# A hybrid decoder step on one core: the last tile's products stand beside the gate matrices, and its retrieval is decoded in small steps

## The chip, the cores and the metric

The kernel runs on one core of one Trainium2 chip. The metric is the device time of one execution in microseconds (us), from the first instruction to the last with what lies around them; three executions of the kernel before are given, and one more that was taken with the profiler on. Engines are called as in the profile: PE is the matrix engine, DVE the vector engine, ACT the scalar engine, POOL the general engine that also issues indirect gathers, SP the engine whose queue issues most plain transfers.

## The reference, cut to what matters

One layer of a decoder is computed for 512 prompt tokens (with 16 learned tokens ahead of them) and for 32 sample tokens. A recurrent group of heads and a window-attention group are computed from one projection, joined, projected by `w_out` and added to x. Then follows the part that matters here, the retrieval of experts (`peer`), and a last norm:

```python
x = x + concat(y_rw, y_at) @ w_out
h = rmsnorm(x, norm2_g)
q = (h @ w_query).reshape(T, 8, 2, 128)            # 8 heads, 2 halves of the key
s = einsum('thcd,cnd->thcn', q, sub_keys)          # 128 scores for each half
s1, i1 = top_k(s[:, :, 0], 16); s2, i2 = top_k(s[:, :, 1], 16)
cand, cidx = s1[..., :, None] + s2[..., None, :], i1[..., :, None] * 128 + i2[..., None, :]
top, sel = top_k(cand, 16)                         # over the 256 pairs of each head
idx, gate = cidx[sel], softmax(top)                # 128 experts for each token, of 16384
act = gelu(h . expert_u[idx]) * gate
y = x + sum_k act[k] * expert_v[idx[k]]            # then rmsnorm(y, final_norm_g)
```

Every matrix is float32: `expert_u` and `expert_v` have 16384 rows of 4 KB each.

## The kernel before, in words

**Stages.** The tokens are 4 tiles of 128 prompt tokens and one of 32 sample tokens. From 0 to about 1110 us runs the front: projections, the recurrent scan, attention, and the heads of tiles 0 to 2 and of the sample. Two ways of retrieval are used. Tiles 1 and 2 (256 tokens) go through **all** experts densely, in 128 blocks of 128 experts; each token's gate is zero for the experts that it didn't choose. Tile 0, the sample and tile 3 (the last) fetch their chosen rows with gathers: 128 gathers of `expert_u` rows and 128 of `expert_v` rows per tile, 512 KB each (32 and 32 for the sample).

**Gates** (1119 to 1238 us, `gates`). The gate matrix (128 tokens by 128 by 128 experts) of each dense tile is made in 16 steps of 8 tokens. DVE and ACT make one-hot rows (uH, uL, vH), PE multiplies them (8 products a step, L1401), ACT copies the results out. The first tile's matrices go to DRAM (gscr), the second's stay (gA, gB) but for a quarter.

**Dense blocks** (1238 to 2184 us). For each block of 128 experts PE transposes its rows (L1446), multiplies them with the hidden states in three products of high and low parts (L1460, L1461, L1463: 24 matmuls), and after gelu (ACT) and gates (DVE) multiplies the result with `expert_v` into PSUM (L1477 to L1479: 24 matmuls). POOL makes the low part vL of `expert_v` once in each block (L1453), so that vL numbers the blocks in a trace. DVE makes uL twice, the gate product twice, and aL once for each block.

**The last tile** (`late`, a generator). Four steps of `w_out` (L1522), the norm, 8 transposes, then 8 steps with two products of `w_query` and two of the scores each (L1544, L1547); after each second one `two_heads` decodes a group of 2 heads: the 16 best of 128 by MAX8, FIND_INDEX8 and MATCH_REPLACE8 on DVE, tables on DVE and POOL. Two steps are traced behind each dense block, from block 0. The four groups done, tile 3's 256 gathers are appended to the work at the side.

**Gathers at the side** (`experts`, L1032, and `beside`). A generator issues a gather on POOL into one of 5 buffers; two gathers later DVE takes the row: for `expert_u` a dot product (`gat<-gat,h` or `gat<-gat,lx`), for `expert_v` an addition (`x<-gat,act,x`). Behind each gate step 0.8 of such a step is traced, behind each dense block up to 3; at the end of the program what is left of them.

**Order.** The framework sorts each engine's instructions at build time by a model of their times, with the tracing order as priority. Each engine then runs its own list in that order and waits where an operand or a buffer isn't ready. A pool of tiles that is opened where an earlier one lay waits for the users of that memory; sb and pp (front) and dn and dp (gates and dense blocks) are such pools. After the dense blocks, `finish` norms and stores tiles 1 and 2, and the last gathers' tile.

Of the kernel before, what the change touches and what calls it, by code (L numbers as in the profile page):

```python
# [11 lines left out]
F32 = mybir.dt.float32  # L12
# [5 lines left out]
PSUM = bass.MemoryType.PSUM  # L18
# [95 lines left out]
def hymba_step(ctx, tc, x_prompt, x_sample, cache_k, cache_v, state_wkv, state_shift, meta, norm1_g, w_in, mu, w0,  # L114
# [3 lines left out]
    A, G, T, DM = nc.scalar, nc.gpsimd, nc.tensor, nc.sync  # L118
# [22 lines left out]
    hscr_s = dr.tile([32, D], F32, name="hscr_s")  # L141
    xscr_s = dr.tile([32, D], F32, name="xscr_s")
    sscr = dr.tile([32, 16, 128], F32, name="sscr")
    yscr = dr.tile([128, 8, 128], F32, name="yscr")
    gscr = dr.tile([16, 128, 128, 8], F32, name="gscr")
    gscr2 = dr.tile([128, 4, 128, 8], F32, name="gscr2")
# [748 lines left out]
    def top16(src, vals, idx):  # L895

        V.max(vals[:, 0:8], src)
        V.max_index(idx[:, 0:8], vals[:, 0:8], src)
        V.match_replace(src, vals[:, 0:8], src, -3.0e38)
        V.max(vals[:, 8:16], src)  # L900
        V.max_index(idx[:, 8:16], vals[:, 8:16], src)

    held = []
# [64 lines left out]
                        eq=("ce", 1), res=("res", 2), d1=("d1", 2))[kind], shape, dt)  # L968

    def two_heads(sc, dst, tile_):  # L970

        vals, idx = tile_("vals", [128, 2, 2, 16]), tile_("idx", [128, 2, 2, 16], U32)
        for j in range(4):
            top16(sc[:, j, :], vals[:, j // 2, j % 2, :], idx[:, j // 2, j % 2, :])
        idf = idx.bitcast(F32)
        V.tensor_copy(idf, idx)
        cand = tile_("cand", [128, 2, 72])  # L980
        for c0, a0_, na, nb in ((0, 0, 2, 16), (32, 2, 2, 8), (48, 4, 4, 4), (64, 8, 8, 1)):
            G.tensor_tensor(cand[:, :, c0:c0 + na * nb].rearrange("p h (a b) -> p h a b", b=nb),
                            bc(vals[:, :, 0, a0_:a0_ + na].unsqueeze(3), [128, 2, na, nb]),
                            bc(vals[:, :, 1, 0:nb].unsqueeze(2), [128, 2, na, nb]), OP.add)

        def sm(dt=F32):
            return tile_("sm", [128, 2, 16], dt)
        top, sel, d1 = tile_("top", [128, 2, 16]), tile_("sel", [128, 2, 16], U32), tile_("d1", [128, 2, 16])
        for h in range(2):
            top16(cand[:, h, :], top[:, h, :], sel[:, h, :])  # L990
        pf = sm()
        V.tensor_copy(pf, sel)
        m = sm()
        V.tensor_scalar(m, pf, 32.0, 8.0, OP.is_ge, OP.mult)
        for lim, x in ((48.0, 4.0), (64.0, 3.0)):
            t = sm()
            V.tensor_scalar(t, pf, lim, x, OP.is_ge, OP.mult)
            V.tensor_tensor(m, m, t, OP.add)
        mu_ = sm(U32)
        V.tensor_scalar(mu_, m, -1.0, 15.0, OP.mult, OP.add)  # L1000
        V.tensor_tensor(sel, sel, mu_, OP.bitwise_and)
        bf = mu_.bitcast(F32)
        V.tensor_copy(bf, sel)
        G.tensor_copy(d1[:, :, 0:1], idf[:, :, 0, 0:1])
        G.tensor_tensor(d1[:, :, 1:16], idf[:, :, 0, 1:16], idf[:, :, 0, 0:15], OP.subtract)
        full = [128, 2, 16, 16]
        res = dst[0:2] if len(dst) == 3 else [tile_("res", [128, 32]) for _ in range(2)]
        for r, tab, pos, op, val in ((res[0], first, pf, OP.is_le, d1), (res[1], iota16, bf, OP.is_equal, idf[:, :, 1, :])):
            eq = tile_("eq", full)
            V.tensor_tensor(eq, bc(tab.unsqueeze(1).unsqueeze(1), full), bc(pos.unsqueeze(3), full), op)  # L1010
            G.tensor_tensor(eq, eq, bc(val.unsqueeze(2), full), OP.mult)
            V.tensor_reduce(r.rearrange("p (h k) -> p h k", h=2), eq, AX.X, OP.add)
        if len(dst) == 2:
            V.scalar_tensor_tensor(dst[0], res[0], 128.0, res[1], OP.mult, OP.add)
        gate = dst[-1].rearrange("p (a b) -> p a b", a=2)
        V.tensor_tensor(gate, top, bc(top[:, :, 0:1], [128, 2, 16]), OP.subtract)
        A.activation(gate, gate, AF.Exp)
        su, rd = small(2, "R"), small(2, "R")
        V.tensor_reduce(su, gate, AX.X, OP.add)
        V.reciprocal(rd, su)  # L1020
        V.tensor_tensor(gate, gate, bc(rd.unsqueeze(2), [128, 2, 16]), OP.mult)
# [139 lines left out]
    with ExitStack() as px:  # L1161
# [43 lines left out]
        def put(src, dst):  # L1205

            A.copy(dst[0], src)
            V.tensor_tensor(dst[1], src, dst[0].bitcast(F32), OP.subtract)
# [68 lines left out]
            project(blk, wt, ws, jps(), lambda k: [t[:, k, :] for t in hA], NA, _t(pj, "own", 2, [128, NA]),  # L1277
                    _t(pj, "po", 3, [128, NA]), 0)

    sb = fr.enter_context(tc.tile_pool(name="sb", bufs=1))  # L1280
    pp = fr.enter_context(tc.tile_pool(name="pp", bufs=1, space=PSUM))
    def meta_wkv():
        r = rwkv_prep(40, 16)
        wkv_local(r)
# [95 lines left out]
    def gates(its, sel, ps, put):  # L1380


        i1T, i2T, gaT = sel
        its, iot = its
        ib = dt_("aH", 2, [128, 2, 128], BF16)
        for c, x in enumerate((i1T, i2T)):
            A.copy(ib[:, c], x)
        for n, t8 in enumerate(range(0, 128, 8)):
            ob = dt_("uL", 2, [128, 128, GA], BF16)
            o0, o1 = dt_("uH", 2, [128, 8, 128]), dt_("vH", 2, [128, 8, 128])  # L1390
            V.tensor_tensor(o0.rearrange("p t j -> p j t"), its, bc(ib[:, 0, t8:t8 + 8].unsqueeze(1), [128, 128, 8]), OP.is_equal)
            V.tensor_tensor(ob, its[:, :, 0:GA], bc(ib[:, 1, t8:t8 + GA].unsqueeze(1), [128, 128, GA]), OP.is_equal)
            for q0 in (0, 4):
                p = ps()
                for q in range(q0, q0 + 4):
                    t = slice(t8 + q, t8 + q + 1)
                    if q < GA:
                        A.mul(o1[:, q, :], ob[:, :, q], gaT[:, t])
                    else:
                        V.tensor_scalar(o1[:, q, :], iot, i2T[:, t], gaT[:, t], OP.is_equal, OP.mult)  # L1400
                    T.matmul(p[:, 128 * (q - q0):128 * (q - q0) + 128], o0[:, q, :], o1[:, q, :], start=True, stop=True)  # L1401
                put(t8 + q0, p)
            with tc.issue_after(marks[-1]):
                beside(RATE_G)


    ND = 256
    dn = ctx.enter_context(tc.tile_pool(name="dn", bufs=1))
    dp = ctx.enter_context(tc.tile_pool(name="dp", bufs=1, space=PSUM))

    def dt_(tag, bufs, shape, dt=F32):
        return _t(dn, tag, bufs, shape, dt)
# [95 lines left out]
    def late():  # L1508
        x2 = dt_("lx", 1, [128, D])
        DM.dma_start(x2, x_prompt[0, 384:512, :])  # L1510
        yT = dt_("ly", 1, [128, 8, 128])
        DM.dma_start(yT, yscr)

        def weights_of(w, n):
            wt = dt_("uv", UV, [128, 8, 256])
            DM.dma_start(wt, w[0][:, 256 * n:256 * n + 256].rearrange("(k p) c -> p k c", p=128))
            return wt
        for n in range(4):
            wt = weights_of(w_out, n)
            p = dps()[:, 0:256]  # L1520
            for k in range(8):
                T.matmul(p, yT[:, k, :], wt[:, k, :], start=(k == 0), stop=(k == 7))  # L1522
            o = x2[:, 256 * n:256 * n + 256]
            V.tensor_tensor(o, o, p, OP.add)
            yield True
        gj = dt_("uv", UV, [128, 2, D])
        DM.dma_start(gj[:, 0], norm2_g[0].partition_broadcast(128))
        DM.dma_start(xscr[3], x2)
        rms(x2, x2, 128, gj[:, 0], "E", gj[:, 1])
        yield True  # L1530
        h2T = dt_("ly", 1, [128, 8, 128])

        def put(half, p):
            A.copy(h2T[:, 4 * half:4 * half + 4, :], p)
        h_transposed(x2, 128, put, dps)
        yield True
        for g in range(4):
            sc = dt_("lsc", 1, [128, 4, 128])
            for j0 in (0, 2):
                wt = weights_of(w_query, 2 * g + j0 // 2)  # L1540
                for j in range(2):
                    p = dps()
                    for k in range(8):
                        T.matmul(p[:, 0:128], wt[:, k, 128 * j:128 * j + 128], h2T[:, k, :], start=(k == 0), stop=(k == 7))  # L1544
                    qT = dt_("lq", 1, [128, 128])
                    A.copy(qT, p[:, 0:128])
                    T.matmul(p[:, 128:256], qT, skT[:, j, :], start=True, stop=True)  # L1547
                    A.copy(sc[:, j0 + j, :], p[:, 128:256])  # L1548
                yield True
            two_heads(sc, [x[:, 32 * g:32 * g + 32] for x in pl1], late_tile)  # L1550
        side.append(tile_experts(3, *pl1, x2))

    for n in range(AHEAD):
# [4 lines left out]
    sels = [sel_transposed(0, dps, dt_("selT", 1, [128, 3, 128])), sel_transposed(1, dps, dt_("lsc", 1, [128, 3, 128]))]  # L1558
    gates(its, sels[0], dps, stage)
    gates(its, sels[1], dps, keep)  # L1560
    gl = {}

    def gate_of(j):
# [68 lines left out]
```

## Time and profile before

| | us |
|---|---|
| median of 3 runs | 2198.62 |
| lowest, highest | 2183.69, 2198.69 |
| profiled execution, its own time | 2204.76 |
| span in the profile | 2203.0 |
| PE busy | 1839.1 (83%) |
| DVE busy | 1690.4 (77%) |
| POOL busy | 1249.2 (57%) |
| ACT busy | 867.3 (39%) |

A page of the profile gives the busy share of each engine in 40 slices of the span (55 us each), the clock that PE was granted, and what the transfers moved. Views of the trace give an engine's instructions in order of time, the busy time of all engines in a stretch, or groups by line; the number in brackets in a timeline is how long the engine stood idle just before, and what ended that. In all of them an instruction on DVE has line 126, since one helper records them; its tiles tell which it is.

### The profile page before, as it was taken

Reading aid. Unit: us, or ns where it says so; the run is one execution under the profiler, and the core shown is the slowest. Engines: PE = TensorE matmul, PEld = TensorE weight load, DVE = VectorE, ACT = ScalarE, POOL = GpSimd, SP = SyncE. Lnnn points to the kernel's source line nnn. Section 1 sums busy time; section 2 is a strip of 40 time slices with the busy share of each in tenths; the row PEclk is TensorE's granted clock in tenths of the full one; section 3 lists DMA queues with packets and bytes.
Section 4 is the critical chain, followed back from the end, with each engine's and each line's share of the span. In section 5 each row is a group of like instructions: output and inputs, shape, how many; then the busy total and the mean of one; then the engine's idle time right before and its main releaser. Section 6 shows DMA issues by size and latency. Waiting matters only on the chain.

```text
span 2203.0 us, 37197 instructions
## 1 busy us (share of the span) xinstructions
PE 1839.1 (83%) x13915; PEld 1716.0 (78%) x13915; DVE 1690.4 (77%) x3393; ACT 867.3 (39%) x1963; POOL 1249.2 (57%) x963
## 2 busy tenths in 40 slices
PE   5899975585759868996547897899999999999996
PEld 5888974473647747886446787899999999999995
DVE  5543436788788788799989879997778787787887
ACT  6554422211224313323169634334444444444443
POOL 0110103878784676565624546867667776767774
PEclk9999996556755659898778999999999999999998
DMA  7532473687786789996757887799899999999995
GB/s 222 157 101 84 122 191 102 208 288 248 230 273 199 231 273 318 285 317 222 243 163 242 299 313 239 270 326 340 334 330 331 342 326 336 335 325 343 325 330 178
DMA packets 310154, 569.51 MB, mean 259 GB/s; under 512 B 32787, under 2 KB 194565, under 8 KB 309830
## 3 DMA queue, kind: packets, MB, share of 16 engines
q0 software_dynamic: 84048, 305.70, 39.7%
q1 hardware_dynamic: 225926, 261.43, 36.6%
q8 instruction: 110, 1.80, 0.3%
q14 instruction: 70, 0.57, 0.1%
HBM read 543.07 MB, written 24.60 MB: 258 GB/s over the span
## 4 chain that ended last, share of the span: by engine, by line
PE 51%; DVE 22%; DMA 10%; issue 9%; POOL 5%; ACT 3%; SPq 0%; DVEq 0%; POOLq 0%; ACTq 0%
DVE gat L126 5%; PE acc L1478 5%; PE w L1460 5%; PE w L1461 5%; PE w L1463 5%; PE acc L1479 5%; PE acc L1477 5%; PE w L1446 4%; POOL gat L1032 4%; DVE x L126 4%; PE pD L218 3%; DMA gat<-in_expert_v_dram,ei 3%; PE ps L218 2%; DMA wst<-in_w_query_dram 2%; DMA gat<-in_expert_u_dram,ei 2%
## 5 line engine op out<-in xcount | busy, mean ns | idle before, releaser
L126 DVE SCALAR_TENSOR_TENSOR x<-gat,act,x 128x1024 f32<-128x1024 f32 x287 | 427.9, 1491 | 24.7 <-DMA gat<-in_expert_v_dram,ei 23.4
L1032 POOL DMA_INDIRECT gat<-in_expert_u_dram,ei x256 | 343.0, 1340 | 158.8 <-DVE pre L126 75.7
L1032 POOL DMA_INDIRECT gat<-in_expert_v_dram,ei x256 | 294.4, 1150 | 193.6 <-DVE x L126 73.1
L1453 POOL TENSOR_TENSOR vL<-uv,vH 128x1024 fp32r<-128x1024 f32 x128 | 322.5, 2519 | 56.1 <-ACT vH L1452 54.3
L1478 PE MATMUL acc<-aL,vH 128*128 128x256 f32 x1024 | 290.7, 289 | 17.2 <-DVE aL L126 17.1
L1479 PE MATMUL acc<-aH,vL 128*128 128x256 f32 x1024 | 289.3, 287 | 0.0
L1477 PE MATMUL acc<-aH,vH 128*128 128x256 f32 x1024 | 280.5, 295 | 5.3 <-ACT aH L1469 5.3
L1460 PE MATMUL w<-dhH,uH 128*128 128x256 f32 x1024 | 252.5, 284 | 0.2 <-ACT lsc L1548 0.2
L1461 PE MATMUL w<-dhL,uH 128*128 128x256 f32 x1024 | 251.6, 283 | 0.0
L126 DVE CUSTOM_DVE_ANT_0 gat<-gat,h 128x1024 f32<-128x1024 f32 x160 | 213.5, 1343 | 49.6 <-DMA gat<-in_expert_u_dram,ei 47.8
L1478 PEld LDWEIGHTS acc<-aL,vH 128*128 128x128 f32 x1024 | 200.6, 196 | 19.3 <-DVE aL L126 19.3
L126 DVE CUSTOM_DVE_ANT_0 gat<-gat,lx 128x1024 f32<-128x1024 f32 x128 | 214.4, 1686 | 0.0
L1452 ACT CAST vH<-uv 128x1024 fp32r<-128x1024 f32 x128 | 134.6, 1051 | 195.7 <-issue 131.8
L1479 PEld LDWEIGHTS acc<-aH,vL 128*128 128x128 f32 x1024 | 200.6, 196 | 0.0
L1460 PEld LDWEIGHTS w<-dhH,uH 128*128 128x128 f32 x1024 | 196.9, 192 | 0.5 <-ACT lsc L1548 0.4
L1461 PEld LDWEIGHTS w<-dhL,uH 128*128 128x128 f32 x1024 | 196.8, 192 | 0.1
L1477 PEld LDWEIGHTS acc<-aH,vH 128*128 128x128 f32 x1024 | 188.0, 193 | 6.0 <-ACT aH L1469 5.9
L126 DVE TENSOR_TENSOR uL<-w,uH 128x512 fp32r<-128x512 f32 x256 | 167.6, 681 | 3.0 <-ACT uH L1448 3.0
L126 DVE TENSOR_TENSOR w<-w,gl 128x128 f32<-128x128 f32 x128 | 50.5, 395 | 143.3 <-ACT w L1464 143.2
L1463 PE MATMUL w<-dhH,uL 128*128 128x256 f32 x1024 | 151.9, 287 | 2.8 <-DVE uL L126 2.8
L1448 ACT CAST uH<-w 128x512 fp32r<-128x512 f32 x256 | 139.1, 592 | 8.4 <-PE w L1446 3.0
L1446 PE MATMUL w<-ident,uv 128*128 128x128 f32 x1024 | 141.4, 273 | 0.0
(575 smaller groups left out, 4113.8 us busy)
## 6 DMA issues: line engine op xcount, KB each, us to landing
uv<-in_expert_u_dram SPq DMA_DIRECT2D x128, 512.0 KB, 4.5
uv<-in_expert_v_dram SPq DMA_DIRECT2D x128, 512.0 KB, 5.9
wst<-in_w_query_dram SPq DMA_DIRECT2D x48, 512.0 KB, 5.5
wst<-in_w_out_dram SPq DMA_DIRECT2D x24, 512.0 KB, 6.9
wst<-in_w_in_dram SPq DMA_DIRECT2D x20, 512.0 KB, 4.4
h2T<-in_w_in_dram SPq DMA_DIRECT2D x20, 512.0 KB, 4.1
gscr<-uv SPq DMA_DIRECT2D x10, 1024.0 KB, 6.5
gl<-gscr SPq DMA_DIRECT2D x16, 512.0 KB, 7.4
```

The costliest lines, as they stand in the source:

```text
L126: r = getattr(nc.vector, name)(*args, **kw)
L1032: G.indirect_dma_start(out=r, out_offset=None, in_=w[0], in_offset=bass.IndirectOffsetOnAxis(ap=ei[:, k:k + 1], axis=0))
L1446: T.transpose(p[:, q, :], un[:, 128 * k:128 * k + 128], ident)
L1448: A.copy(uH[:, ks, :], p)
L1452: A.copy(vH, vn)
L1453: G.tensor_tensor(vL, vn, vH.bitcast(F32), OP.subtract)
L1460: T.matmul(pre, uH[:, k, :], hH[:, k, :], start=(k == 0), stop=False)
L1461: T.matmul(pre, uH[:, k, :], hL[:, k, :], start=False, stop=False)
L1463: T.matmul(pre, uL[:, k, :], hH[:, k, :], start=False, stop=(k == 7))
L1477: T.matmul(o, vH[:, ds_], aH, start=(j == 0 and d % 2 == 0), stop=False, skip_group_check=True)
L1478: T.matmul(o, vH[:, ds_], aL, start=False, stop=False, skip_group_check=True)
L1479: T.matmul(o, vL[:, ds_], aH, start=False, stop=(j == 127), skip_group_check=True)
```

## The change

Three things. First, `late` is one step for each step of `gates`, so that its products stand beside the 16 steps of the first gate matrix; the scores go to buffers of the tag gl, and from there to DRAM (lscr, 256 KB a group). Second, decoding is now `late_heads`: a group's scores are read back from lscr, and `head_steps` decodes them in pieces (7 yields a group, 28 in all), two pieces behind each dense block; then tile 3's gathers follow as before. Third, pools sb, pp, dn and dp wait tile by tile for the memory that they take over.

```diff
+    lscr = dr.tile([4, 128, 4, 128], F32, name="lscr")
...
     def two_heads(sc, dst, tile_):
+        for _ in head_steps(sc, dst, tile_):
+            pass
+
+    def head_steps(sc, dst, tile_):
...
             top16(sc[:, j, :], vals[:, j // 2, j % 2, :], idx[:, j // 2, j % 2, :])
+            if j % 2:
+                yield True
...
             top16(cand[:, h, :], top[:, h, :], sel[:, h, :])
+        yield True
...
         G.tensor_tensor(d1[:, :, 1:16], idf[:, :, 0, 1:16], idf[:, :, 0, 0:15], OP.subtract)
+        yield True
...
             V.tensor_reduce(r.rearrange("p (h k) -> p h k", h=2), eq, AX.X, OP.add)
+            yield True
...
-    sb = fr.enter_context(tc.tile_pool(name="sb", bufs=1))
-    pp = fr.enter_context(tc.tile_pool(name="pp", bufs=1, space=PSUM))
+    sb = fr.enter_context(tc.tile_pool(name="sb", bufs=1, reuse_waits="tile"))
+    pp = fr.enter_context(tc.tile_pool(name="pp", bufs=1, space=PSUM, reuse_waits="tile"))
...
                 put(t8 + q0, p)
+            next(more, None)
             with tc.issue_after(marks[-1]):
                 beside(RATE_G)
...
-    dn = ctx.enter_context(tc.tile_pool(name="dn", bufs=1))
-    dp = ctx.enter_context(tc.tile_pool(name="dp", bufs=1, space=PSUM))
+    dn = ctx.enter_context(tc.tile_pool(name="dn", bufs=1, reuse_waits="tile"))
+    dp = ctx.enter_context(tc.tile_pool(name="dp", bufs=1, space=PSUM, reuse_waits="tile"))
...
-            sc = dt_("lsc", 1, [128, 4, 128])
+            sc = dt_("gl", 2, [128, 4, 128])
...
-            two_heads(sc, [x[:, 32 * g:32 * g + 32] for x in pl1], late_tile)
+            DM.dma_start(lscr[g], sc)
+        held[:] = [x2]
+
+    def late_heads():
+        for g in range(4):
+            sc = dt_("lsc", 1, [128, 4, 128])
+            DM.dma_start(sc, lscr[g])
+            yield from head_steps(sc, [x[:, 32 * g:32 * g + 32] for x in pl1], late_tile)
+            yield True
+        x2, = held
         side.append(tile_experts(3, *pl1, x2))
...
     gates(its, sels[1], dps, keep)
+    for _ in more:
+        pass
+    more = late_heads()
```

On PE the first gate steps stood alone; w are PSUM tiles, vH and uH the one-hot rows, L1401 the gates' products, and x4 counts matmuls:

```order
L1401 MATMUL w_8925<-vH_8922,uH_8921 128x128 x4
L1401 MATMUL w_8936<-vH_8922,uH_8921 128x128 x4
L1401 MATMUL w_8951<-vH_8948,uH_8947 128x128 x4
L1401 MATMUL w_8961<-vH_8948,uH_8947 128x128 x4
L1401 MATMUL w_8980<-vH_8977,uH_8976 128x128 x4
```

In the changed program the line of the gates' products is L1411, of `w_out` L1533, of `w_query` L1555 and of the scores L1558. The same place on PE (from the first gate product, and a little further on):

```order
L1411 MATMUL w_8926<-vH_8923,uH_8922 128x128 x4
L1411 MATMUL w_8937<-vH_8923,uH_8922 128x128 x4
L1533 MATMUL w_8953<-uv_8951,ly_8949 128x256 x8
L1411 MATMUL w_8968<-vH_8965,uH_8964 128x128 x4
L1411 MATMUL w_8978<-vH_8965,uH_8964 128x128 x4
```
```order
L1555 MATMUL w_9199<-ly_9157,uv_9197 128x128 x8
L1555 MATMUL w_9212<-ly_9157,uv_9197 128x128 x8
L1411 MATMUL w_9233<-vH_9230,uH_9229 128x128 x3
L1558 MATMUL w_9199<-skT,lq_9208 128x128
L1411 MATMUL w_9233<-vH_9230,uH_9229 128x128
L1411 MATMUL w_9243<-vH_9230,uH_9229 128x128 x4
```

All the products of the last tile (4 times 8 of `w_out`, 8 transposes, 16 times 8 of `w_query`, 16 of scores) stand so between the 128 products of the first gate matrix; the 128 of the second follow without them, and so do the dense blocks.

On POOL the program's end was this (L1453 is a block's vL, L1032 a gather, L1063 a transfer of the last norm's weights):

```order
L1453 TENSOR_TENSOR vL_21325<-uv_21305,vH_21324 128x1024
L1032 DMA gat_18624<-in_expert_v_dram,ei_11_105 128x1024
L1032 DMA gat_18627<-in_expert_v_dram,ei_11_105 128x1024
L1032 DMA gat_18709<-in_expert_v_dram,ei_11_105 128x1024
L1453 TENSOR_TENSOR vL_21404<-uv_21384,vH_21403 128x1024
L1032 DMA gat_18712<-in_expert_v_dram,ei_11_105 128x1024
L1032 DMA gat_18715<-in_expert_v_dram,ei_11_105 128x1024
L1063 DMA gat_18800<-in_final_norm_g_dram 128x1024
```

In the changed program (L1464 and L1042 are the same lines) the last vL has 17 gathers behind it, of which the first ones and the last one stand here:

```order
L1042 DMA gat_18835<-in_expert_v_dram,ei_11_106 128x1024
L1464 TENSOR_TENSOR vL_21417<-uv_21397,vH_21416 128x1024
L1042 DMA gat_18838<-in_expert_v_dram,ei_11_106 128x1024
L1042 DMA gat_18841<-in_expert_v_dram,ei_11_106 128x1024
...
L1042 DMA gat_19283<-in_expert_v_dram,ei_11_106 128x1024
L1073 DMA gat_19368<-in_final_norm_g_dram 128x1024
```

Before, the first gather of tile 3 stood behind the vL of block 8, and 2 were left behind the last; now the first one stands behind that of block 10, five of them before block 14, and 17 are left. On DVE the first dot product for tile 3 stood behind the aL of block 7 and now stands behind that of block 14; the decoding of the four groups and 18 additions of the sample lie ahead of it.

## Rows read from the trace of the kernel before

**Rows 1.** The page, part 2: PE's busy tenths in 40 slices.
```profile
PE   5899975585759868996547897899999999999996
```

**Rows 2.** Table by stretch; columns stand in the first row.
```profile
core 0: us, PE busy (x) PEld busy (x) DVE busy (x) ACT busy (x) POOL busy (x), PEclk, DMA share, GB/s
1500.00:2100.00 600.00, 600.00 (x5078) 600.00 (x5077) 470.93 (x726) 253.08 (x456) 434.81 (x275) 1.00 0.92 334
1124.80:1180.40 55.60, 40.47 (x252) 37.49 (x253) 53.49 (x84) 51.37 (x128) 15.78 (x13) 0.83 0.77 231
1180.40:1238.30 57.90, 37.17 (x257) 33.99 (x256) 57.90 (x76) 55.44 (x191) 29.75 (x13) 0.91 0.73 244
1238.50:1403.70 165.20, 142.42 (x1085) 138.09 (x1084) 136.98 (x377) 65.61 (x138) 92.91 (x80) 0.95 0.84 290
1403.70:1507.60 103.90, 98.21 (x798) 96.18 (x798) 97.58 (x150) 40.40 (x72) 77.28 (x48) 0.98 0.86 302
1250.00:1300.00 50.00, 46.47 (x328) 44.20 (x328) 32.49 (x48) 16.41 (x33) 24.55 (x16) 0.97 0.98 344
```

**Rows 3.** Timeline of POOL (start, us): vL of blocks 0, 13, 27, 127.
```profile
1238.51 2.37 POOL L1453 TENSOR_TENSOR vL<-uv,vH 128x1024 fp32r<-128x1024 f32 x1 [0.85 <-ACT vH L1452]
...
1403.66 2.48 POOL L1453 TENSOR_TENSOR vL<-uv,vH 128x1024 fp32r<-128x1024 f32 x1 [1.25 <-ACT vH L1452]
...
1507.60 2.41 POOL L1453 TENSOR_TENSOR vL<-uv,vH 128x1024 fp32r<-128x1024 f32 x1
...
2175.04 2.72 POOL L1453 TENSOR_TENSOR vL<-uv,vH 128x1024 fp32r<-128x1024 f32 x1
```

**Rows 4.** Timeline of DVE: the front's last reduction, first gate instruction.
```profile
1109.94 0.69 DVE L126 TENSOR_REDUCE dsel<-ce 128x32 f32<-128x512 f32 x1 [1.44 <-POOL ce L1011]
...
1119.60 0.59 DVE L126 TENSOR_SCALAR vH<-aL,selT 128x128 f32<-128x128 f32 x2
```

**Rows 5.** Timeline of PE: transposes of hscr and dsel, first gate products.
```profile
1114.57 3.65 PE L1426 MATMUL w<-ident,uv 128*128 128x128 f32 x16 [33.62 <-DMA uv<-hscr]
1118.01 1.49 PE L1368 MATMUL w<-ident,dsel 128*128 128x128 f32 x6
1124.81 8.50 PE L1401 MATMUL w<-vH,uH 128*128 128x128 f32 x48 [5.31 <-ACT vH L1398]
```

**Rows 6.** Groups by line on PE, 1238 to 1420: busy us, mean ns | idle.
```profile
L1544 PE MATMUL w<-ly,uv 128*128 128x128 f32 x256 | 32.4, 284 | 6.4 <-DVE uL L126 4.6 <-ACT lsc L1548 1.8
...
L1522 PE MATMUL w<-uv,ly 128*128 128x256 f32 x64 | 14.1, 379 | 0.0
L1547 PE MATMUL w<-skT,lq 128*128 128x128 f32 x32 | 6.3, 281 | 0.0
...
L182 PE MATMUL w<-ident,lx 128*128 128x128 f32 x8 | 1.1, 279 | 1.5 <-DVE lx L126 1.5
```

**Rows 7.** Groups by line and shape on DVE, 1238 to 1407.
```profile
L126 DVE SCALAR_TENSOR_TENSOR x<-gat,act,x 128x1024 f32<-128x1024 f32 x19 | 32.0, 1684 | 0.1
L126 DVE CUSTOM_DVE_ANT_0 gat<-gat,lx 128x1024 f32<-128x1024 f32 x14 | 22.3, 1614 | 0.0
...
L126 DVE TENSOR_TENSOR lx<-lx,w 128x256 f32<-128x256 f32 x4 | 1.7, 414 | 3.9 <-PE w L1522 3.9
...
L126 DVE SCALAR_TENSOR_TENSOR lx<-lx,sE,uv 128x1024 f32<-128x1024 f32 x1 | 1.3, 1271 | 0.0
```

**Rows 8.** Timeline of POOL: a gather behind the last vL.
```profile
2177.91 1.75 POOL L1032 DMA_INDIRECT gat<-in_expert_v_dram,ei  x1 [0.16 <-issue]
```

**Rows 9.** Timeline of POOL: first and last of 13 gathers in a row.
```profile
734.98 1.02 POOL L1032 DMA_INDIRECT gat<-in_expert_v_dram,ei  x1 [0.30 <-issue]
...
753.28 0.94 POOL L1032 DMA_INDIRECT gat<-in_expert_v_dram,ei  x1 [0.58 <-DVE x L126]
```

**Rows 10.** The chain of waits: start, duration, the last gather's landing.
```profile
2179.97 6.70 DMA gat<-in_expert_v_dram,ei
```

**Rows 11.** Timeline of DVE: the last addition.
```profile
2186.76 1.28 DVE L126 SCALAR_TENSOR_TENSOR x<-gat,act,x 128x1024 f32<-128x1024 f32 x1 [0.93 <-DMA gat<-in_expert_v_dram,ei]
```

## The prediction

> **What bounds the kernel now.** I read the page's slices first, then a table by stretch, then timelines of single engines. In the slices [rows 1] PE is full from slice 28 to the end: the dense blocks are bound by PE there. The table [rows 2] says it exactly: from 1500 to 2100 us PE is busy 600.00 of 600 at clock 1.00, DVE 470.93. The vL of a block numbers the blocks: from block 27 (1507.60) to block 127 (2175.04) they take 667.44 us [rows 3], so a block costs 6.67 us. Before that PE is not the bound. In the gates [rows 2] DVE is busy 53.49 of 55.6 us in the first half (first matrix) and 57.90 of 57.9 in the second, while PE is idle 15.1 and 20.7 us. Blocks 0 to 13 take 165.2 us, of which PE is busy 142.4 (the last tile's products among them) and DVE 137.0; blocks 13 to 27 take 103.9, where fourteen at 6.67 would take 93.4. Behind the last vL stand 28.0 us (2175.04 to the span's end, 2203.0).
>
> So the change moves PE work from a stretch where PE is nearly full to one where it is not, and must be followed in five stretches. The sum is made against the profiled execution, 2204.76 us; the median of the runs shown is 6.1 less, and I put the shift on the median.
>
> **1. Start of the gates (tile-wise waits): -6.6 us.** Before, the transfer that reads hscr was issued only when the front's last reduction was over (1109.94 + 0.69 = 1110.63 [rows 4]); PE stood idle 33.62 us until it landed, made 16 transposes from 1114.57, then those of dsel at 1118.01 [rows 5], and DVE began at 1119.60 [rows 4]. In the changed order the hscr part no longer waits for that reduction; dsel does. The gates then begin the same 1.6 us behind the dsel transposes, at about 1113. For the pools sb and pp I take nothing: what is first read there waits for a transfer's data, not for the pool. If a further wait on memory shows up at dn, the 6.6 is lost; the bounds are -7 and 0.
>
> **2. Gates with the last tile's products: +43 us.** What is added on PE [rows 6]: 14.1 (w_out) + 32.4 (w_query) + 6.3 (scores) + 1.1 (transposes) = 53.9 us, all in the first half, since the order puts one step behind each of its 16 gate steps. With the 40.47 that PE has there, 94.4 us if it is never idle, in place of 55.6: +38.8. Idle time remains where the norm lies between w_out and the transposes, and where a score waits for ACT's copy of its query: between 0 and 12 us, I take 4, since the rows show only 1.5 before the transposes, and gate products stand between a query product and its score. ACT gets its copies too; it is busy 51.4 of 55.6 now, and has 94 later. SP gets 12 loads of 1 MB, some of them queued behind stores of gate matrices. This half moves 231 GB/s in 55.6 us, 12.8 MB; with 12 MB of weights and 1 MB of scores it is 25.8 MB in 98 us, 263 GB/s, below the 344 that a stretch reached [rows 2], so the loads are hidden if each starts a step or two early. The stores of the scores and their reading back are 256 KB each, and the reading waits for nothing recent: nothing. The second half stays DVE's, 57.9. Bounds: +39 and +51.
>
> **3. Blocks 0 to 13: -42 us.** PE loses the 53.9 and would need 13 x 6.67 = 87. DVE does not lose as much: from its 137.0 go the 14 dot products (22.3), which now come behind the decoding, and the sums and the norm's last step on lx (1.7 + 1.3) [rows 7]; the decoding, cut in pieces, is the same instructions. 18 additions remain of 19 (1.7 less), and the decoding that lay behind the stretch comes in, which I set against that with 3 us. That leaves 113 us of DVE work: **DVE, not PE, is the bound of these blocks**, at 8.7 us each. Its idle time was 28.2 us here; part of that waited for the last tile's products (3.9 for w_out [rows 7]) and falls away. I take 10 us, so 123 in place of 165.2. DVE works in order: a dense block's uL or gate product queues behind a decoding step or behind an addition whose gather is late, and PE waits for it. Bounds of the idle: 5 and 28.
>
> **4. Blocks 13 to 27: -6.5; 27 to 127: 0.** The 10.5 us over PE's pace came with the end of the decoding and a burst of gathers. The decoding is over by then; the burst (32 gathers in 13 blocks by the new order, 2.46 a block) stays. At 512 KB a gather and 1 MB a block this is 2.34 MB, and at 344 GB/s [rows 2] 6.8 us a block: 3 us over fifteen blocks. I leave 4 of the 10.5; bounds 0 and 10.5. From there on PE bounds both kernels.
>
> **5. Behind the last vL: +18 us.** Two gathers stood there, now 17. The first went out 2.87 us behind the vL's start [rows 3, 8]. Thirteen gathers in a row took 18.30 us from first to last issue, 1.53 each [rows 9], 344 GB/s again; 16 more take 24.4 us. The last lands 6.70 later [rows 10], its addition takes 1.28 [rows 11]. From the last addition's end to the span's end were 15.0 us (2188.04 to 2203.0), in which three tiles were normed; two of them now get theirs while the gathers run, so I take 11 for one (bounds 8 and 15). Sum 2.9 + 24.4 + 6.7 + 1.3 + 11 = 46.3 against 28.0. The bounds of a gather, 1.3 (an issue of 1.02 and 0.30 between [rows 9]) and 1.9 (1.75 and 0.16 [rows 8]), give +12 and +28.
>
> The Trainium skill (DMA: Bandwidth & Descriptors, the table of bandwidths at its head) gives about 358 GB/s as what one core gets from HBM. By it a gather would cost 1.46 us and this step 1.0 us less; the row's 344 is nearer to what this kernel does, and is used.
>
> **Sum:** -6.6 + 43 - 42 - 6.5 + 0 + 18 = +6 us. Said in one line, the shift is DVE's idle time in blocks 0 to 13 less 4. On the profiled execution 2211, on the median **2205 us**. This is no change that can be told: runs of this kernel lie 15 us apart, and within 1% (2177 to 2221) I call the same.
>
> **Rivals.** *Slower: DVE's queue stalls the first blocks.* The place is DVE in blocks 0 to 13; the mechanism is that each block's uL, gate product and aL stand behind decoding and additions in one queue, PE's results come later for it, and DVE then waits for PE and ACT in turn, as it does now. For it speaks that of the 28.2 us idle now the rows put only 3.9 to w_out's products, which leave. Against it, that decoding in small pieces gives DVE something else to do from the first block. If the idle stays at 28 the shift is +24: 2223 us; with the gates at their upper bound 2231. It decides from an idle of 26 us on.
>
> *Faster: the products hide in the gates.* PE is idle there, 35.8 us in both halves, and each engine keeps working in the blocks. PE never idle in the first half gives +39, idle of 5 in the blocks -47, no excess to block 27 -10.5, the tail at its lower bound +12, the start -7: -13, so 2185. If besides the additions fall from their mean of 1.68 us to the 1.28 of one without vL beside it [rows 7, 11], 18 x 0.4 = 7 more, 2178; a further shortening of the decoding would be needed to go below. The rows speak against most of it, since one half of the gates takes all 53.9 and has 15.1 of room.
>
> The Trainium skill (Perfetto Trace Analysis, Optimization Strategy) says that where the busiest engine changes over a kernel's time, interleaving the stretches can help, which is this rival. The rows agree on the change of engine and not on the room.
>
> *The change doesn't do what it says:* the tile-wise waits move nothing, because another wait stands behind the one that goes. That costs the 6.6 of step 1: 2212, inside the forecast.
>
> **Chances and range.** The forecast, within 1%: 0.57 (the last rival's 0.1 is in it). Slower by over 1%: 0.26, from the stalls and the long tail together, since each alone only just reaches it. Faster by over 1%: 0.17, which needs several steps at their good ends at once, or a cost that I see twice. Range 2178 to 2236: the low end is the faster rival with its shorter additions, the high end the stalls with the gates at their bound and some of the tail's.
>
> **What would show it.** Gates: DVE begins near 1113; first gate product to first vL about 157 us instead of 114 [rows 3, 5], with PE busy over 90% in the first half. Blocks 0 to 13 by their vL near 123 us, with DVE busy over 90% and PE under 75%. Blocks 27 to 127 at 6.67 us. Behind the last vL 17 gathers about 1.5 us apart, and 46 us to the end. I am wrong if the first half of the gates stays under 80 us, if blocks 0 to 13 take over 145 or under 110, or if the gathers at the end are done before PE's last product.

## The result, and the profile after

The changed kernel takes 2225.93 us (median of 4, 2217.0 to 2229.64); the kernel before takes 2198.65 in the runs beside it. The ratio is 1.0135, with an interval of 1.0097 to 1.0174: slower, by 27 us on the medians. The forecast was 2205 (no change, 2177 to 2221); the range 2178 to 2236 holds the result, the case that came is the slower one. The profiled executions stand 18.2 us apart (2204.76 and 2222.97).

To see where, I cut both profiled executions at the same events: the end of the front's last reduction (dsel), the first and the 129th gate product on PE (the matrices' halves), the vL of blocks 0, 13, 27 and 127, and the span's end. Times in us, worked out from start times in the timelines:

| stretch | before | after | difference | forecast |
|---|---|---|---|---|
| span's start to the last reduction's end | 1110.6 | 1107.1 | -3.5 | 0 |
| from there to the first gate product | 14.2 | 7.5 | -6.7 | -6.6 |
| first half of the gates | 56.9 | 117.3 | **+60.4** | +43 |
| second half, to the vL of block 0 | 56.8 | 57.6 | +0.8 | 0 |
| blocks 0 to 13 | 165.2 | 119.7 | -45.5 | -42 |
| blocks 13 to 27 | 103.9 | 95.7 | -8.2 | -6.5 |
| blocks 27 to 127 | 667.4 | 668.0 | +0.6 | 0 |
| behind the last vL | 28.0 | 48.3 | +20.3 | +18 |
| sum | 2203.0 | 2221.2 | +18.2 | +6 |

The start of the gates, DVE's and PE's timeline of the changed kernel (start, duration, operation, idle time ahead in brackets):

```profile
1106.42 0.69 DVE L126 TENSOR_REDUCE dsel<-ce 128x32 f32<-128x512 f32 x1 [1.44 <-POOL ce L1020]
...
1109.41 0.59 DVE L126 TENSOR_SCALAR vH<-aL,selT 128x128 f32<-128x128 f32 x2
```
```profile
1087.55 1.97 PE L1437 MATMUL w<-ident,uv 128*128 128x128 f32 x8 [0.51 <-DMA uv<-hscr]
1107.76 1.54 PE L1378 MATMUL w<-ident,dsel 128*128 128x128 f32 x6 [18.24 <-DVE dhL L126]
1114.61 3.50 PE L1411 MATMUL w<-vH,uH 128*128 128x128 f32 x16 [5.31 <-ACT vH L1408]
```

Where [rows 4, 5] had the transposes of hscr behind the last reduction, they now stand 20 us ahead of it; DVE's gates begin 2.3 us behind its end in place of 9.0.

The table by stretch of the changed kernel answers to [rows 2], with the columns named there; the rows are its dense blocks, the two halves of the gates, and blocks 0 to 13 and 13 to 27:

```profile
1500.00:2100.00 600.00, 599.88 (x5070) 599.55 (x5070) 476.53 (x740) 251.46 (x453) 440.77 (x275) 1.00 0.92 333
1114.60:1231.90 117.30, 90.80 (x616) 86.66 (x617) 60.18 (x93) 64.96 (x174) 19.26 (x13) 0.86 0.70 223
1231.90:1289.60 57.70, 37.55 (x265) 34.65 (x266) 56.42 (x74) 55.18 (x193) 30.71 (x14) 0.91 0.70 237
1289.60:1409.30 119.70, 97.40 (x727) 95.15 (x726) 113.06 (x350) 51.98 (x90) 69.24 (x67) 0.89 0.70 240
1409.30:1504.90 95.60, 95.00 (x791) 93.83 (x791) 85.67 (x139) 39.88 (x71) 73.76 (x44) 1.00 0.85 311
```

In the first half of the gates no engine is full: PE is busy 90.8 of 117.3, DVE 60.2, ACT 65.0. That is a chain of waits, not an engine that is the bound. Nor is it the bytes: 223 GB/s over 117.3 us are 26.2 MB, the prediction had 25.8, at a rate below the 344 of [rows 2]. Blocks 0 to 13 are DVE's, busy 113.06 of 119.7. What PE waits for in that half (total, times, longest):

```profile
PE w L1555 <- DMA uv<-in_w_query_dram: 12.8, 4, 3.9
PE w L183 <- DVE lx L126: 9.0, 1, 9.0
PE w L1411 <- ACT vH L1408: 5.3, 1, 5.3
PE w L1533 <- DMA uv<-in_w_out_dram: 4.4, 1, 4.4
```

17.2 us are for weights, 9.0 for the norm. The chain of waits shows why the weights are late; this is one round of it, from a gate product (L1411) to the loads behind the next store of gate matrices (start, duration, what; SPq is SP's queue, uv a staging buffer):

```profile
1170.64 1.13 PE w L1411 x10
1171.77 0.02 issue
1171.79 0.59 ACT uv L1499
1172.39 0.02 issue
1172.40 0.37 SPq L1501
1172.77 0.04 issue
1172.81 9.10 DMA uv<-in_w_query_dram
1181.92 0.14 issue
1182.05 5.44 PE w L1555 x32
1187.49 0.89 PE w L1411 x8
...
1190.15 0.37 SPq L1501
1190.52 0.05 issue
1190.57 8.61 DMA uv<-in_w_query_dram
```

A gate product ends, ACT copies it, SP's store of the gate matrices (L1501) was waiting for that copy and goes, and only then the two loads of `w_query` queued behind it on SP go, 0.4 us later. The product can start 9.10 us later, when they have landed; in PE's order it stands ahead of the next gate products. So the next copy, the next store and the next loads wait for these. One round is 17.75 us (1172.40 to 1190.15) for two gate steps, where the second half, which is DVE's, takes 7.2 for two (57.6 for 16). On the chain of this half stand five such loads, one of `w_out` (8.42 us) and four of `w_query` (11.24, 9.10, 8.61 and 8.52).

And the tail, answering to [rows 8, 11], POOL's first and last gathers behind the last vL (17 in all), and DVE's last addition:

```profile
2175.76 1.76 POOL L1042 DMA_INDIRECT gat<-in_expert_v_dram,ei  x1
2177.83 1.16 POOL L1042 DMA_INDIRECT gat<-in_expert_v_dram,ei  x1 [0.30 <-issue]
...
2205.48 1.86 POOL L1042 DMA_INDIRECT gat<-in_expert_v_dram,ei  x1 [0.76 <-DVE x L126]
```
```profile
2211.86 1.28 DVE L126 SCALAR_TENSOR_TENSOR x<-gat,act,x 128x1024 f32<-128x1024 f32 x1 [1.37 <-DMA gat<-in_expert_v_dram,ei]
```

16 intervals in 29.7 us are 1.86 each, over the 1.53 that I took and near the bound of 1.9; from the last addition's end (2213.14) to the span's end are 8.1, at the other bound.

### The profile page after: what moved, and what is told of

Same layout as the page of the kernel before. It is cut to its first block, busy times and chain, and to the rows that moved or that the text cites. A ratio compares the mean times of both kernels' runs of the same rounds, so it can differ in the third digit from the quotient of the medians.

```text
span 2221.2 us, 37214 instructions
## 1 busy us (share of the span) xinstructions
PE 1845.0 (83%) x13915; PEld 1722.5 (78%) x13915; DVE 1682.3 (76%) x3393; ACT 865.6 (39%) x1962; POOL 1256.9 (57%) x963
## 4 chain that ended last, share of the span: by engine, by line
PE 49%; DVE 20%; DMA 11%; issue 10%; POOL 6%; ACT 3%; SPq 0%; POOLq 0%; DVEq 0%; ACTq 0%
DVE x L126 5%; PE w L1474 4%; PE w L1471 4%; PE w L1472 4%; PE acc L1489 4%; PE acc L1490 4%; PE acc L1488 4%; POOL gat L1042 4%; PE w L1457 4%; PE pD L219 3%; DVE gat L126 3%; DMA gat<-in_expert_u_dram,ei 3%; DMA gat<-in_expert_v_dram,ei 2%; DMA wst<-in_w_query_dram 2%; PE ps L219 2%
## 5 line engine op out<-in xcount | busy, mean ns | idle before, releaser
L126 DVE SCALAR_TENSOR_TENSOR x<-gat,act,x 128x1024 f32<-128x1024 f32 x287 | 447.3, 1559 | 29.2 <-DMA gat<-in_expert_v_dram,ei 27.9
L1042 POOL DMA_INDIRECT gat<-in_expert_v_dram,ei x256 | 317.7, 1241 | 189.0 <-DVE x L126 73.2
L1042 POOL DMA_INDIRECT gat<-in_expert_u_dram,ei x256 | 330.8, 1292 | 155.4 <-DVE pre L126 75.8
L1464 POOL TENSOR_TENSOR vL<-uv,vH 128x1024 fp32r<-128x1024 f32 x128 | 320.6, 2505 | 62.5 <-ACT vH L1463 60.5
L126 DVE CUSTOM_DVE_ANT_0 gat<-gat,lx 128x1024 f32<-128x1024 f32 x128 | 178.1, 1405 | 1.5 <-DMA gat<-in_expert_u_dram,ei 1.5
L126 DVE TENSOR_TENSOR w<-w,gl 128x128 f32<-128x128 f32 x128 | 50.8, 397 | 129.4 <-ACT w L1475 129.2
L1459 ACT CAST uH<-w 128x512 fp32r<-128x512 f32 x256 | 138.7, 592 | 12.8 <-PE w L1457 7.7
```

Of the source, the lines that this page charges most:

```text
L126: r = getattr(nc.vector, name)(*args, **kw)
L1042: G.indirect_dma_start(out=r, out_offset=None, in_=w[0], in_offset=bass.IndirectOffsetOnAxis(ap=ei[:, k:k + 1], axis=0))
L1459: A.copy(uH[:, ks, :], p)
L1464: G.tensor_tensor(vL, vn, vH.bitcast(F32), OP.subtract)
```

## The experiments

Theories: the loads' place in a queue behind the stores of gate matrices makes the first half of the gates long (first Q, then L in the expectations, which differ in what mends it); against it, that the staging buffers are too few (B), that the work fits on PE only if it is spread over both halves (H), or that interleaving costs by itself. The other terms are tried by the first and third run.

**Tile-wise waits alone**, on the kernel before:

```diff
-    dn = ctx.enter_context(tc.tile_pool(name="dn", bufs=1))
+    dn = ctx.enter_context(tc.tile_pool(name="dn", bufs=1, reuse_waits="tile"))
```
(and so for sb, pp and dp)

> The kernel before with nothing but the tile-wise waits of the four pools; every engine's order is that of before. Theory: the transposes of hscr leave the path between the front's last reduction and the gates, so the gates begin about 2.3 us behind that reduction's end in place of 9.0, and the whole is 6 to 8 us faster than before, about 2192. Rival: another wait takes their place, and the time stays within 2 us of before.

Measured 2193.39, ratio 0.9956 (0.993 to 0.9981), 7 us on the medians. From the last reduction's end to the first gate product are 7.5 us as in the changed kernel, and every later stretch keeps its length within 1.5 us but blocks 0 to 13 (161.8, 3.4 less). DVE's rows:

```profile
1114.59 0.69 DVE L126 TENSOR_REDUCE dsel<-ce 128x32 f32<-128x512 f32 x1 [1.44 <-POOL ce L1011]
1115.19 2.47 DVE L126 TENSOR_TENSOR dhL<-w,dhH 128x512 fp32r<-128x512 f32 x4
1117.58 0.59 DVE L126 TENSOR_SCALAR vH<-aL,selT 128x128 f32<-128x128 f32 x2
```

This part of the change is a gain of its own size. It is the only part that was tried without the rest.

**The weight loads on POOL's queue**, on the changed kernel:

```diff
-            DM.dma_start(wt, w[0][:, 256 * n:256 * n + 256].rearrange("(k p) c -> p k c", p=128))
+            G.dma_start(wt, w[0][:, 256 * n:256 * n + 256].rearrange("(k p) c -> p k c", p=128))
```

> The changed kernel with the 12 weight loads of the last tile issued from POOL's queue in place of SP's, where each pair stood behind a store of a gate matrix. Theory Q (the SP queue holds the loads back): the 17.2 us in which PE waits for weights in the first half of the gates shrink to under 6, that half takes 100 to 106 us in place of 117.3, and the whole is 10 to 16 us faster than the changed kernel. Rival B (the loads wait for one of the 5 staging buffers, whichever queue they are in): the half stays at 113 to 120 us, the loads go out as late as now, and the gathers behind them on POOL come later; the whole is the same or slower. The 9.0 us in which PE waits for the norm stay in both.

Measured 2226.06, ratio 1.0104 (1.0069 to 1.0138): no gain over the changed kernel, and the first half takes 114.4 us. The sizes are the rival's, its reason isn't. `w_out`'s wait is gone, but PE still waits 15.3 us for `w_query`. POOL's timeline shows what the loads now stand behind:

```profile
1176.49 1.07 POOL L1042 DMA_INDIRECT gat<-in_expert_v_dram,eis  x1 [12.17 <-DVE pre L126]
1177.56 1.88 POOL L1527 DMA_DIRECT2D uv<-in_w_query_dram  x2
1196.65 1.09 POOL L1042 DMA_INDIRECT gat<-in_expert_v_dram,eis  x1 [17.21 <-DVE pre L126]
1197.73 1.81 POOL L1527 DMA_DIRECT2D uv<-in_w_query_dram  x2
```

Each pair goes out right behind a gather that had waited 12 and 17 us for DVE, and DVE had waited for PE's gate products just before (9.26 and 11.03 us, 46.8 in the whole half):

```profile
1172.69 1.97 DVE L126 TENSOR_TENSOR uH<-vL,aH 128x1024 f32<-128x1024 bf16 x1 [9.26 <-PE w L1411]
1192.85 1.97 DVE L126 TENSOR_TENSOR uH<-vL,aH 128x1024 f32<-128x1024 bf16 x1 [11.03 <-PE w L1411]
```

That is the same ring through another queue. Only two loads have PE's products as releaser, as one that waits for a buffer would (12.8 us at a load of `w_out` that was early anyway, 4.6 at one of `w_query`). So it isn't SP that is at fault but the load's place behind something that waits for the gate step. The 2.9 us that the half gains are more than lost in blocks 0 to 13, which take 129.5 in place of 119.7.

**Four pieces of the decoding for each block**, on the changed kernel:

```diff
-LATE = 2
+LATE = 4
```

> The changed kernel with four pieces of the decoding behind each dense block in place of two. By the order 10 gathers are left behind the last vL in place of 17. Theory (the tail goes by the gathers left): the time behind the last vL shrinks by 7 x 1.6 = 11 us to about 37, the blocks 0 to 13 stay bound by DVE, and take up to 8 us more since some dot products come into them, which blocks 13 to 27 give back: 8 to 12 us faster than the changed kernel. Rival (DVE's first blocks pay for it): blocks 0 to 27 lose what the tail gains, within 3 us of the changed kernel.

Measured 2223.0, ratio 1.0095 (1.0055 to 1.0134), 3 us under the changed kernel's median; between the two nothing can be told. In the stretches both halves of the theory are there but for the giving back: behind the last vL 35.9 us in place of 48.3, blocks 0 to 13 125.4 in place of 119.7, and blocks 13 to 27 103.3 in place of 95.7. DVE's work comes back where it is the bound (blocks 0 to 13 and 13 to 27, columns as above):

```profile
1263.80:1389.20 125.40, 101.13 (x759) 97.48 (x759) 117.42 (x353) 52.96 (x93) 76.97 (x70) 0.91 0.70 240
1389.20:1492.50 103.30, 94.39 (x759) 92.58 (x759) 88.36 (x151) 40.01 (x70) 72.93 (x50) 0.97 0.89 323
```

The tail goes by the gathers left (12.4 us for 7), and starting them sooner moves that cost ahead rather than away: the rival's outcome.

**One step behind every second gate step**, on the changed kernel:

```diff
-            next(more, None)
+            if n % 2 == 0:
+                next(more, None)
```

> The changed kernel with one step of the last tile behind every second gate step, so that its 53.9 us of PE work lie in both halves of the gates. Theory H (PE has room for it only if it is spread): a half then has 64 to 68 us of PE work against DVE's 57, the gates take 130 to 142 us from the first product to the last in place of 174, and the whole is 25 to 40 us faster than the changed kernel, so 5 to 15 us faster than before. Rival (what costs is the interleaving itself, by waits of each step on loads and on ACT's copies, wherever it is put): the gates stay over 160 us and the whole within 12 us of the changed kernel.

Measured 2249.81, ratio 1.0225 (1.0183 to 1.0266): 24 us slower than the changed kernel. My expectation was plainly wrong. The gates take 203.9 us from the first product to the last, as the rival had it (over 160), but the whole is slower than the rival's 12 us allow. PE's timeline and SP's, at the second load of `w_out`:

```profile
1108.13 3.73 PE L1411 MATMUL w<-vH,uH 128*128 128x128 f32 x32
1119.76 6.69 PE L1534 MATMUL w<-uv,ly 128*128 128x256 f32 x16 [7.89 <-DMA uv<-in_w_out_dram]
```
```profile
1110.73 0.38 SPq L1502 DMA_DIRECT2D gscr<-uv  x1
1111.21 1.92 SPq L1528 DMA_DIRECT2D uv<-in_w_out_dram  x1
```

PE now waits for seven of the twelve loads in place of five, and 8.8 us each time in place of 3.4 (32.1 us for `w_query`, 29.6 for `w_out`). The rows show why a wait is longer: the load goes out at 1111.21, the products that PE still has end at 1111.86, and it stands idle until the load has landed. What costs is the rounds, and how little work of PE lies between a load and its product, not the room on PE, as the run with both edits shows below.

**Each load two steps ahead of its products**, on the changed kernel:

```diff
+        todo = [(w_out, n) for n in range(4)] + [(w_query, n) for n in range(8)]
+        loaded = [weights_of(*todo.pop(0)) for _ in range(2)]
+        def next_weights():
+            if todo:
+                loaded.append(weights_of(*todo.pop(0)))
+            return loaded.pop(0)
...
-            wt = weights_of(w_out, n)
+            wt = next_weights()
...
-                wt = weights_of(w_query, 2 * g + j0 // 2)
+                wt = next_weights()
```

> The changed kernel, with each of the 12 weight loads traced two steps of the last tile ahead of its products. Theory L (a load is let go by the store of the gate step just ahead of its products, and PE then waits for its landing): the 17.2 us in which PE waits for weights in the first half of the gates fall under 4, that half takes 99 to 104 us in place of 117.3, the second stays at 57, and the whole is 12 to 18 us faster than the changed kernel. The 9 us for the norm stay. Rival (buffers: with two loads in flight the gate steps wait for the same 5 staging buffers): the waits move to ACT's copies of the gate matrices and their stores, and the half stays over 110 us.

Measured 2197.93, ratio 1.0002 (0.9964 to 1.004): 28 us faster than the changed kernel (12 to 18 were expected) and level with before. The waits of PE in the first half, and the two halves in the table by stretch (columns as above):

```profile
PE w L183 <- DVE lx L126: 8.9, 1, 8.9
PE w L1411 <- ACT vH L1408: 5.3, 1, 5.3
```
```profile
1115.10:1204.10 89.00, 79.95 (x616) 77.92 (x616) 60.41 (x93) 64.90 (x174) 19.30 (x13) 0.93 0.83 271
1204.10:1261.70 57.60, 36.99 (x264) 34.10 (x265) 56.37 (x74) 55.22 (x193) 30.63 (x13) 0.91 0.71 238
```

No wait for weights is left, with the same 5 buffers and the same queue: this settles L against B. The first half takes 89.0 us, less than the 99 to 104 of theory L: the gain is larger than the 17.2 us of waiting, since the same 616 records on PE also take 79.95 us in place of 90.80, at a granted clock of 0.93 in place of 0.86.

**Both: spread over both halves, loads ahead**, the norm's weights one step ahead too (the edits of the last two runs together, and the load of the norm's weights moved up):

```diff
             wt = next_weights()
+            if n == 3:
+                gj = dt_("uv", UV, [128, 2, D])
+                DM.dma_start(gj[:, 0], norm2_g[0].partition_broadcast(128))
             p = dps()[:, 0:256]
...
-        gj = dt_("uv", UV, [128, 2, D])
-        DM.dma_start(gj[:, 0], norm2_g[0].partition_broadcast(128))
```

> One step of the last tile behind every second gate step, as in the run that spread it over both halves, with each weight load two steps ahead and the norm's weights one step. Theory L: of the 203.9 us from the first gate product to the last in that run, the 61.7 of waiting for weights go to under 8, the norm's 9.4 to about 3, and the gates take 132 to 145 us (PE has 64 to 68 us of work in each half); the whole is 28 to 42 us faster than the changed kernel, thus 5 to 20 faster than before. Rival (waits of ACT and DVE on PE's late steps, one for the other, hold each gate step longer wherever the weights are): the gates stay over 160 us, and the whole is no faster than before.

Measured 2179.59, ratio 0.9932 (0.9897 to 0.9966): faster than before by 20 us on the medians and than the changed kernel by 46, a little more than the theory's 42. The gates take 130.6 us to the vL of block 0 (129.4 to their last product):

```profile
1116.10:1186.60 70.50, 59.45 (x399) 56.45 (x400) 60.71 (x96) 59.82 (x151) 23.16 (x14) 0.87 0.87 280
1186.60:1246.70 60.10, 58.03 (x484) 55.32 (x482) 55.49 (x70) 57.54 (x211) 21.59 (x12) 1.00 0.94 319
```

H holds once loads are early: 16.0 us less than with all work in one half (146.6). The norm's wait is 8.2, so loading its weights sooner did little for it.

**The same with four pieces of decoding:**

```diff
-LATE = 2
+LATE = 4
```

> The run with spread steps and early loads, and four pieces of decoding behind each block; 11 gathers are left behind the last vL in place of 17. Theory (DVE is the bound until about block 27, and dot products that come in there cost what the tail gains): the tail 9 to 11 us shorter, blocks 0 to 27 9 to 13 longer, the whole within 4 us of the run with two pieces (2180). Rival (the blocks have slack now that the gates end early): 8 us or more faster than that run.

Measured 2175.51, ratio 0.9896 (0.9833 to 0.9959); its interval overlaps that of two pieces, so it isn't told apart. By stretches of the profiled executions: tail 40.2 in place of 49.1, blocks 13 to 27 99.3 in place of 93.0, blocks 0 to 13 122.0 in place of 124.2. So blocks 0 to 27 give up 4.1 us, not the 9 to 13 of the theory, against 8.9 gained in the tail; a gain of 5 us would fit, and the runs don't show it. The median is the lowest of the study, but this run and the next are from another chip, where the kernel before took 2194.81: it stands 19 us under that, the run with two pieces 20 us under its own (2199.63).

**The same, with 310 steps of the side work in the front**, on the last run:

```diff
-AHEAD = 280
+AHEAD = 310
```

> As the run with spread steps, early loads and four pieces, and 310 steps of the side work in place of 280 in the front, so that no addition of the sample is left behind the gates, tile 3's gathers begin behind block 9, and 3 are left behind the last vL. Theory (DVE's work up to block 27 is conserved; it only helps where DVE is idle now): about 18 additions and 12 dots of 1.2 to 1.5 us, some 35 us, go into the front, where DVE is busy 196 of the last 210 us: the front becomes 15 to 35 us longer, blocks 0 to 27 some 20 to 30 shorter and the tail 18 shorter, so 5 to 25 us faster than the run with spread steps and early loads. Rival (the front's path hides none of it): the front grows by 35 or more, and the whole is the same.

Measured 2183.89, ratio 0.9963 (0.9931 to 0.9995). Against the run with spread steps and early loads (49.1, 124.2 and 93.0) the tail is 29.0 us, blocks 0 to 13 take 108.6 and 13 to 27 94.1: 20 us less in the tail, as expected, and 14.5 in the blocks, where 20 to 30 were. But against the last run the front's last reduction ends at 1131.5 in place of 1110.6 and the gates begin 15.7 us behind it in place of 7.5, which is 29 us where the rival had 35 or more. The whole is the rival's. What is taken from a stretch where DVE is the bound and put into another of that kind is not gained.

## Why the prediction was right or wrong

**Start of the gates:** right, -6.7 for -6.6, and the run with that part alone shows it by itself. That sb and pp bring nothing to the front is not shown: its end lay at 1083.0 to 1115.3 us in runs that have no edit there.

**Gates with the last tile's products: the step that failed.** +61 us for +43, beyond the bound of +51. The PE work was sized too large if anything (94.4 us for 90.8 busy, and 80.0 once nothing waits for weights); the idle time was 26.5 us for 4, so PE was busy 77% of the half and not over 90%. What failed is the sentence that the loads are hidden if each starts a step or two early, with 4 us of idle time. I had seen that loads stand behind stores, and weighed only bytes against bandwidth. The chain above shows that a load is issued behind a store that waits for the very gate step before its products, so that its whole way, 8.4 to 11.2 us, lies on the chain in each of five rounds; the run with loads two steps ahead takes that away and 28 us with it. Of these, 17.2 are waits for weights, and 10.9 are that PE's own instructions took longer. The norm was undersized too: PE waited 9.0 us there, where the rows of before showed 1.5.

**Blocks 0 to 13:** right, -45.5 for -42; DVE was busy 113.06 us, where I had 113, and its idle time was 6.6 for 10. PE was busy 97.4 us, where I had 87 from the blocks' later pace: 81%, not under 75%, at a granted clock of 0.89. With that the slower rival is refuted as a mechanism, though its side came: its place was DVE's idle time in these blocks, which fell from 28.2 to 6.6.

**Blocks 13 to 127:** right, -8.2 and +0.6 for -6.5 and 0.

**Behind the last vL:** +20.3 for +18, by two errors that partly cancel: 1.86 us for a gather in place of 1.53 (5.3 us more in all; POOL waits for DVE in several of these intervals, which may be why), and 8.1 us for the end in place of 11.

**The faster rival** needed room in the gates; the spread run with early loads shows that the room is there, in both halves. The Trainium skill (Perfetto Trace Analysis, Optimization Strategy) says that interleaving stretches with different busiest engines may help; the traces agree only with loads that are early, where the gates and blocks 0 to 13 take 254.8 us in place of 278.9 before, and not without, where they take 294.7 in the changed kernel and 330.9 when spread. The rival that the change does nothing fell with the first step.

**The number:** +6 forecast, +18 in the profiled executions and +27 on the medians. The first gap is the second step (+18), less the front's 3.5 and small differences elsewhere. The second, 9 us, is within what the front varies by from run to run, but no trace of the other runs shows that it is that. That the range holds the result is luck in part: its high end was made of stalls of DVE that didn't come, with the gates at a bound that they passed. None of the three signs named for being wrong came, since none of them was a gate half that takes too long.

## What to carry to other kernels

When work is moved into idle time, follow its loads, not only its instructions: find what stands ahead of each load in its queue, and what that waits for. If it waits for the work next to which the load is to be used, every step costs a full round of copy, store, load and product. More distance between load and use removed it here; another queue did not, since there too the loads stood behind something that waited for the same step (a queue without such waits was not tried). And where one engine is the bound over two neighbouring stretches, moving its work between them shows as a gain in one view and returns in the next: cut the whole run into stretches before believing one of them.

## What the runs showed of the hardware that I had not expected

A wait of PE costs more than itself, since the granted clock falls with it. In the changed kernel the 16 records of a `w_out` product took 6.23 us behind a wait of 4.43 us, and 3.62 when nothing was waited for. The last two rows are the table by stretch for the first 3 us of the slow product and for the fast one: clock 0.50 (1.2 GHz) and 1.00 (2.4 GHz):

```profile
1133.02 6.23 PE L1533 MATMUL w<-uv,ly 128*128 128x256 f32 x16 [4.43 <-DMA uv<-in_w_out_dram]
1139.09 1.95 PE L1411 MATMUL w<-vH,uH 128*128 128x128 f32 x16
1140.87 3.62 PE L1533 MATMUL w<-uv,ly 128*128 128x256 f32 x16
```
```profile
1133.00:1136.00 3.00, 2.98 (x7) 2.46 (x8) 0.00 (x0) 0.00 (x0) 0.00 (x0) 0.50 1.10 369
1140.87:1144.33 3.46, 3.46 (x19) 3.05 (x17) 2.85 (x4) 2.76 (x7) 2.60 (x1) 1.00 0.45 140
```

The same holds for `w_query`: four times 32 records took 5.44 us behind a wait, at a clock of 0.68, and 3.87 in the run with early loads behind none. These five products make some 9 of the 10.9 us. The clock fell six times in this half, each time in one of PE's six waits for weights or the norm or within 1.2 us behind it, and rose again while PE worked; with early loads it fell once, in the wait for the norm. The clock of the whole half was 0.86 with the waits for weights and 0.93 without them, and PE's busy time 90.80 and 79.95 us. Step 2 of the prediction took the durations of the added products from a stretch at 0.95 [rows 2] and had nothing for that.

The front ends at 1083.0 us in one profiled run and at 1115.3 in another, though neither has an edit there beside the tile-wise waits; this spread is as wide as the effects in question. Part of it goes with PE's clock: from 690 to 730 us the run that ended its front at 1083.0 was granted 0.83, the changed kernel (1107.1) 0.50, and the same instructions of DVE in the same order, the 961st to the 1021st, took 60.2 us and 73.6, so 13.4 of the 24.1 us between the two. Why the clock differs there, and the rest, stay open. Comparisons by stretches, counted from the last reduction, are free of it, though each is of one execution: 1092.4 us from there to the end before, 1114.1 for the changed kernel, 1080.7 for the tile-wise waits alone, 1067.2 for the best of those that leave the front's work as it was.
